# Sums of weights pinned behind the work written ahead of them, in a float32 encoder that multiplies by Strassen's scheme

## The chip, the cores and the metric

The kernel runs on one core of a Trainium2 chip. The metric is the device time of one execution in microseconds. A core has five engines that work through queues of their own, in the order in which the program lists their instructions, and meet only at semaphores: TensorE (PE, matmuls; its weight loads are shown as PEld), VectorE (DVE), ScalarE (ACT), GpSimd (POOL) and SyncE (SP, which here only issues DMAs). TensorE accumulates in PSUM; all else lives in SBUF.

## The reference

Two token groups (256 and 512 tokens, width 1024) go through the same two layers in float32. A layer is

```
x <- LN1(alpha*x + 0.5*SwiGLU_1(x))
x <- LN2(alpha*x + W_out[ attention(x) | ssd(x) ])
x <- LN3(alpha*x + 0.5*SwiGLU_2(x))
SwiGLU(x) = (silu(x @ w_gate) * (x @ w_up)) @ w_down      # 1024 -> 2816 -> 1024
```

The middle step has neighbourhood attention and a bidirectional state-space scan. The change touches only the four SwiGLU blocks, which take most of the time.

## The kernel before

**Precision.** A float32 product is made of three faster ones. Each operand is cut into a high part (a cast to fp32r) and a low part (what is left), and high x high, high x low and low x high are added in PSUM. `parts` cuts a block of weights: ScalarE casts the high half (L101 or L105); the low half is made by VectorE (L106) or, where `acc` is set, by ScalarE writing minus the high half (L102) and a DMA from POOL's queue that adds the raw block to it (L103). A cut block lies in one of twelve places, w0 to w4 for gate and up, w5 to w11 for down.

**Pairs.** The 2816 hidden columns are worked in eleven pairs of 128-column tiles. `plain_pair` does the first. `fast_pair` does the other ten by a Strassen scheme: seven products of quarter matrices for gate (m=0) and seven for up (m=1) instead of eight each, in the order of `PRODUCTS`. A product is twelve matmuls of 128x384 at L524. Three of the seven use raw quarters of the weights (0, 1, 3) and four use sums of them, S1 to S4, which `WeightStream.source` makes on VectorE at L89 (S1 = 2+3, S2 = S1-0, S3 = 0-2, S4 = 1-S2) into one of three temporary blocks. On the side of x the partners are quarters of x (XH, XL) and sums of those (T1 to T4 with halves T2h, T2l and so on). A product's weights are cut four products ahead: `ws.get(1, NGU-1)`.

After the last product `finish` makes sums of the hidden quarters (L445 to L448) and `put_h` cuts them (L434 on ScalarE, L436 on VectorE) into h0 to h6.

**Down.** In pairs 1 to 8 the down projection goes by the same scheme, one pair late: `down_units` has 21 runs (three column blocks of seven products, in the order h0, h1, h3, h4, h6, h5, h2), and `fast_pair` of the next pair does one or two behind each of its products. A run is three matmuls of 128x512 (L596) and one or two accumulations into y on VectorE (L599). h0, h4, h5 and h2 share one bank of PSUM (psB), h3 and h6 another (psC): h4's matmuls wait until VectorE has read h0's result, h6's until it has read h3's. `down_step` makes the weights of down: T1, T3, T2 and -T4 are sums in place in the raw blocks (L126, L130, L128, L132), and seven casts cut them, the last of them (into w11) the block that -T4 left.

**Raw weights.** They come in halves of a slab, 512 KB a DMA on SP's queue (L71), into four buffers `wraw`: for each pair two halves of gate, two of up, two of down. A load starts when its buffer's last reader is done.

**Who sets the order.** The kernel is written in program order, and a scheduler then sets the order of each engine's queue. It keeps all dependencies, and among instructions that have none it goes by its own estimate of when operands are ready; it also hands out the buffers of `wraw`. So a sum whose weights it takes to have landed can come ahead of work that is written before it.

Of the kernel before, what the change touches and what calls it, by code (L numbers as in the profile page):

```python
# [36 lines left out]
UNIT = 512  # L37
# [13 lines left out]
class WeightStream:  # L51
# [7 lines left out]

    SUMS = {"S1": (2, "add", 3), "S2": ("S1", "sub", 0), "S3": (0, "sub", 2), "S4": (1, "sub", "S2")}  # L60

    def __init__(self, nc, pool, halves, units, temps, places):
        self.nc, self.pool, self.halves, self.units, self.temps, self.places = nc, pool, halves, units, temps, places
        self.raw, self.sums = {}, {}
        self.ndma = self.nsplit = self.nget = self.nsum = 0
# [14 lines left out]
    def source(self, u, what, n):  # L80
        if not isinstance(what, str):
            return self.block(u["at"][what], n)
        key = (u["at"][0], what)
        if key not in self.sums:
            a, op, b = self.SUMS[what]
            a, b = self.source(u, a, n), self.source(u, b, n)
            out = self.temps[self.nsum % len(self.temps)]
            self.nsum += 1
            (self.nc.vector.tensor_add if op == "add" else self.nc.vector.tensor_sub)(out, a, b)  # L89
            self.sums[key] = out  # L90
        return self.sums[key]

# [28 lines left out]
    def down_step(self, half, step):  # L121

        b11, b12, b21, b22 = (self.block((half + k // 2, k % 2)) for k in range(4))
        sub = self.nc.vector.tensor_sub
        if step == "T1":
            sub(b11, b12, b11)  # L126
        elif step == "T3":
            sub(b12, b22, b12)  # L128
        elif step == "T2":
            sub(b11, b22, b11)  # L130
        elif step == "-T4":
            sub(b21, b21, b11)  # L132
        else:
            hl = self.parts((b11, b21, b11, b11, b22, b12, b21)[step], NGU + step, acc=step not in (0, 2))
            if step >= 5:
                self.dma(half + step - 1)
            return hl
# [9 lines left out]
def trunk(ctx, tc, x_in, w_gu, w_dn, w_xbc, w_z, w_qk, w_v, w_out, ln_gb, ln_gbc, conv_wb, gmix, smalls, bias, y_out):  # L147
    nc = tc.nc
# [3 lines left out]
    wpool = ctx.enter_context(tc.tile_pool(name="wpool", bufs=1))  # L152
# [10 lines left out]
    def at(off, n, dt=F32):  # L163
        a = arena[:, off : off + n]
        return a if dt == F32 else a.bitcast(dt)
# [28 lines left out]
    o_sum, o_s, o_sg = 24 * KB, 30 * KB, 36 * KB  # L194
# [3 lines left out]
    halves, units = [], []  # L198
# [77 lines left out]
                u["place"] = NGU + k if k < NDN else NGU - 1  # L276
            ring[0] = NGU - 1 if w == 1 else NW - 1
    wt = [pers.tile([P, 2 * ZN], F32R, name=f"w{i}") for i in range(NW)]
    ws = WeightStream(nc, wpool, halves, units, [at(o_sum + i * UNIT, UNIT) for i in range(3)], wt)

    y = at(o_y, NT * DM).rearrange("p (t d) -> p t d", t=NT)
    gb = at(o_gb, 2 * DM).rearrange("p (s d) -> p s d", s=2)
# [959 lines left out]
```

## Time and profile before

| | us |
|---|---|
| median of 3 runs | 2982.32 |
| lowest, highest | 2973.87, 2982.59 |
| the profiled execution's own time | 2994.69 |
| its span | 2992.5 |
| TensorE busy | 2883.1 |
| VectorE busy | 2191.0 |
| ScalarE busy | 1583.4 |

The profile is of one execution. Busy time is a union over an engine's instructions; a matmul's end is modelled, so TensorE's share is no measure of its speed. The timeline view gives start, duration, engine, line and operation; in square brackets stands how long the engine had been idle before and what ended that. In the windows view PEclk is the granted share of TensorE's clock (1.00 is 2.4 GHz, 0.50 is 1.2 GHz).

### The profile page before, as it was taken

What the parts mean: (1) busy time and instruction counts of PE and PEld (TensorE: products, weight loads), DVE (VectorE), ACT (ScalarE), POOL (GpSimd) and SP (SyncE); (2) the same over time, 40 slices, a digit from 0 to 9 for tenths busy, and PEclk for the clock granted to TensorE, in tenths of its full rate; (3) what the DMA queues carried; (4) which work ended last, traced back from release to release, by engine and by line L of the source; (5) the groups of instructions that cost most, each with busy time, mean ns of one, the idle gap of its engine ahead of it and who ended that gap; (6) DMA issues with size and microseconds to landing.
All of it is one profiled execution on the core that took longest, in us unless ns stands there. A gap on an engine that the chain in (4) does not pass through costs nothing.

```text
span 2992.5 us, 41957 instructions
## 1 busy us (share of the span) xinstructions
PE 2883.1 (96%) x15094; PEld 2534.0 (85%) x15094; DVE 2191.0 (73%) x4207; ACT 1583.4 (53%) x3231; POOL 408.8 (14%) x513
## 2 busy tenths in 40 slices
PE   8999999999999999999989999999999999999998
PEld 7988889888767888888979888898887778888897
DVE  7777777768435877777797778877783458887877
ACT  4645454657345455554545455545573464554543
POOL 2112120100000211121031121200000002121210
PEclk9999999999889999999999999999997999999999
DMA  3555453224323255554215554632343233454642
GB/s 122 126 121 126 114 127 114 99 88 137 111 62 125 81 134 110 128 128 112 85 36 122 125 126 114 140 100 102 99 124 114 76 122 92 113 132 109 135 106 77
DMA packets 128880, 330.26 MB, mean 110 GB/s; under 512 B 14816, under 2 KB 27296, under 8 KB 127904
## 3 DMA queue, kind: packets, MB, share of 16 engines
q1 hardware_dynamic: 82592, 243.68, 25.6%
q0 software_dynamic: 46080, 83.91, 16.4%
q8 instruction: 118, 1.93, 0.3%
q14 instruction: 90, 0.74, 0.1%
HBM read 224.67 MB, written 18.97 MB: 81 GB/s over the span
## 4 chain that ended last, share of the span: by engine, by line
PE 71%; DVE 11%; DMA 7%; issue 6%; POOL 3%; ACT 2%; POOLq 0%; DVEq 0%; SPq 0%; ACTq 0%
PE psA L524 28%; PE psB L596 7%; PE psA L1119 5%; PE psA L407 5%; PE psA L965 5%; PE psC L596 4%; DMA w<-wraw 4%; DMA wraw<-in_w_gu_dram 3%; PE psB L1054 3%; PE psB L618 3%; PE psC L618 3%; PE psA L772 2%; PE psA L992 2%; DVE arena L599 2%; PE psC L1083 2%
## 5 line engine op out<-in xcount | busy, mean ns | idle before, releaser
L524 PE MATMUL psA<-XH,w 128*128 128x384 f32 x2560 | 700.4, 338 | 5.3 <-DMA w<-wraw 5.3
L524 PEld LDWEIGHTS psA<-XH,w 128*128 128x128 f32 x2560 | 468.6, 188 | 14.4 <-DMA w<-wraw 6.6
L103 POOL DMA_DIRECT2D w<-wraw x320 | 273.8, 881 | 1322.9 <-ACT w L102 1168.0
L524 PE MATMUL psA<-XL,w 128*128 128x384 f32 x1280 | 432.6, 338 | 0.0
L105 ACT CAST w<-arena 128x512 fp32r<-128x512 f32 x320 | 198.4, 620 | 390.2 <-PE psA L524 357.4
L105 ACT CAST w<-wraw 128x512 fp32r<-128x512 f32 (+1 forms) x320 | 194.6, 620 | 214.4 <-PE psA L524 103.9
L106 DVE TENSOR_TENSOR w<-wraw,w 128x512 fp32r<-128x512 f32 (+1 forms) x320 | 216.0, 688 | 110.1 <-ACT w L105 106.3
L599 DVE SCALAR_TENSOR_TENSOR arena<-psB,arena 128x512 f32<-128x512 f32 x384 | 260.7, 686 | 45.5 <-PE psB L596 45.5
L106 DVE TENSOR_TENSOR w<-arena,w 128x512 fp32r<-128x512 f32 x320 | 219.6, 687 | 66.4 <-ACT w L105 66.4
L524 PEld LDWEIGHTS psA<-XL,w 128*128 128x128 f32 x1280 | 240.7, 188 | 7.5
L101 ACT CAST w<-wraw 128x512 fp32r<-128x512 f32 x320 | 197.4, 618 | 92.8 <-PE psA L524 56.5
L407 PE MATMUL psA<-XH,w 128*128 128x256 f32 (+1 forms) x1056 | 241.5, 335 | 5.0 <-DVE XH L372 5.0
L102 ACT ACTIVATE w<-w 128x512 fp32r<-128x512 f32 x320 | 198.8, 631 | 5.7
L599 DVE SCALAR_TENSOR_TENSOR arena<-psC,arena 128x512 f32<-128x512 f32 x288 | 191.7, 684 | 3.3
L407 PEld LDWEIGHTS psA<-XH,w 128*128 128x128 f32 x1056 | 168.6, 189 | 27.0 <-DVE XH L372 6.3
L524 PE MATMUL psA<-T4h,w 128*128 128x384 f32 x640 | 183.6, 348 | 0.0
L524 PE MATMUL psA<-T3h,w 128*128 128x384 f32 x640 | 181.1, 344 | 0.0
L524 PE MATMUL psA<-T2h,w 128*128 128x384 f32 x640 | 177.4, 338 | 0.0
L89 DVE TENSOR_TENSOR arena<-wraw 128x512 f32<-128x512 f32 x160 | 109.4, 686 | 91.9 <-DMA wraw<-in_w_gu_dram 81.6
L539 DVE TENSOR_TENSOR arena<-arena,psA 128x384 f32<-128x384 f32 x240 | 132.0, 550 | 56.9 <-PE psA L524 50.3
L330 POOL TENSOR_TENSOR stat<-stat,cst 128x1 f32<-128x1 f32 x60 | 25.7, 429 | 1033.2 <-ACT arena L933 415.7
L407 PE MATMUL psA<-XL,w 128*128 128x256 f32 (+1 forms) x528 | 151.1, 335 | 2.0 <-DVE XL L373 2.0
(359 smaller groups left out, 6356.0 us busy)
## 6 DMA issues: line engine op xcount, KB each, us to landing
wraw<-in_w_gu_dram SPq DMA_DIRECT2D x176, 512.0 KB, 3.8
w<-wraw POOLq DMA_DIRECT2D x320, 256.0 KB, 4.1
wraw<-in_w_dn_dram SPq DMA_DIRECT2D x88, 512.0 KB, 3.7
e<-ac_d SPq DMA_DIRECT2D x48, 256.0 KB, 3.3
wraw<-in_w_xbc_dram SPq DMA_DIRECT2D x16, 512.0 KB, 4.7
wraw<-in_w_qk_dram SPq DMA_DIRECT2D x16, 512.0 KB, 3.9
arena<-in_bias_dram SPq DMA_DIRECT2D x64, 128.0 KB, 2.1
wraw<-in_w_out_dram SPq DMA_DIRECT2D x16, 512.0 KB, 4.2
```

Of the source, the lines that this page charges most:

```text
L101: nc.scalar.copy(hi, raw)
L102: nc.scalar.activation(lo, hi.bitcast(F32), AF.Copy, scale=-1.0)
L103: nc.gpsimd.dma_start(lo, raw, accum_op=ALU.add)
L105: nc.scalar.copy(hi, raw)
L106: nc.vector.tensor_sub(lo, raw, hi.bitcast(F32))
L407: t_.matmul(ps[:, o : o + b - a], w[:, k % 4], xx[:, k, a:b], start=(k == 0 and part == 0 and i == 0), stop=(k == KD - 1 and part == 1))
L524: t_.matmul(ps, wx[:, k], xx[:, k], start=first and k == 0 and i == 0, stop=k == 3 and i == 2, skip_group_check=not first)
L596: t_.matmul(ps, hx, wx, start=first and k == 0, stop=k == 2, skip_group_check=not first)
L599: v_.scalar_tensor_tensor(sl, ps, 0.5, sl, op0=ALU.mult, op1=ALU.add)
L618: t_.matmul(ps[n], hx, units[2 * i + n][wx], start=(i == 0 and wi == 0), stop=(i == nf - 1 and wi == 2))
L965: t_.matmul(ps[r][:, : b - a], w[:, k % 4], xx[:, k, a:b], start=(k == 0 and part == 0 and i == 0), stop=(k == KD - 1 and part == 1))
L1119: t_.matmul(p[n], xx[:, k, cols], wo[2 * k + n][wx], start=(i == 0 and wi == 0), stop=(i == KD - 1 and wi == 2))
```

## The change

Two kinds of VectorE instruction get one edge more: every sum of weights (L89) and the sum -T4 (L132). The edge, `keep_in_program_order`, puts the instruction behind the one that was traced before it on VectorE. It is an order of issue and adds no wait. Nothing is added or left out, each engine has the same instructions as before, and lines from 63 on have a number one higher.

```diff
-    def __init__(self, nc, pool, halves, units, temps, places):
+    def __init__(self, tc, pool, halves, units, temps, places):
+        nc, self.in_order = tc.nc, tc.keep_in_program_order
...
-            (self.nc.vector.tensor_add if op == "add" else self.nc.vector.tensor_sub)(out, a, b)
+            self.in_order((self.nc.vector.tensor_add if op == "add" else self.nc.vector.tensor_sub)(out, a, b))
...
-            sub(b21, b21, b11)
+            self.in_order(sub(b21, b21, b11))
...
-    ws = WeightStream(nc, wpool, halves, units, [at(o_sum + i * UNIT, UNIT) for i in range(3)], wt)
+    ws = WeightStream(tc, wpool, halves, units, [at(o_sum + i * UNIT, UNIT) for i in range(3)], wt)
```

The scheduler's order follows from it. Below, `arena` holds the temporary sums, the hidden sums and y; numbers at the end of a name are those of the built program. wraw_2704 and wraw_2730 are the halves of gate (m=0) of pair 7 in the first SwiGLU block, wraw_2869 and wraw_2894 those of up (m=1), wraw_2532 and wraw_2551 those of down of pair 6.

VectorE's queue at the end of pair 6, before:

```order
L543 TENSOR_TENSOR arena_66<-arena_66 128x384
L89 TENSOR_TENSOR arena_66<-wraw_2730,arena_66 128x512
L445 TENSOR_TENSOR arena_66<-arena_66 128x384
L89 TENSOR_TENSOR arena_66<-wraw_2869,wraw_2894 128x512
L446 TENSOR_TENSOR arena_66<-arena_66 128x384
L436 TENSOR_TENSOR h3l_186<-arena_66,h3h_185 128x384
L447 TENSOR_TENSOR arena_66<-arena_66 128x384
L436 TENSOR_TENSOR h5l_190<-arena_66,h5h_189 128x384
L448 TENSOR_TENSOR arena_66<-arena_66 128x384
L436 TENSOR_TENSOR h4l_188<-arena_66,h4h_187 128x384
L539 TENSOR_TENSOR arena_66<-arena_66,psA_2928 128x384
L436 TENSOR_TENSOR h6l_192<-arena_66,h6h_191 128x384
```

The same place now, up to the first accumulation of a down run:

```order
L544 TENSOR_TENSOR arena_66<-arena_66 128x384
L446 TENSOR_TENSOR arena_66<-arena_66 128x384
L447 TENSOR_TENSOR arena_66<-arena_66 128x384
L448 TENSOR_TENSOR arena_66<-arena_66 128x384
L437 TENSOR_TENSOR h3l_186<-arena_66,h3h_185 128x384
L449 TENSOR_TENSOR arena_66<-arena_66 128x384
L437 TENSOR_TENSOR h4l_188<-arena_66,h4h_187 128x384
L437 TENSOR_TENSOR h5l_190<-arena_66,h5h_189 128x384
L437 TENSOR_TENSOR h6l_192<-arena_66,h6h_191 128x384
L90 TENSOR_TENSOR arena_66<-wraw_2704 128x512
L540 TENSOR_TENSOR arena_66<-arena_66,psA_2928 128x384
L600 SCALAR_TENSOR_TENSOR arena_66<-psB_2948,arena_66 128x512
```

S4 of m=0 (wraw_2730) and S1 of m=1 (wraw_2869, wraw_2894) have left the middle of `finish`; S3 of m=0 stands behind it, S4 some rows further, S1 and S2 of m=1 behind the seventh accumulation.

VectorE's queue some rows earlier, at the end of the product T4 of pair 6, before:

```order
L132 TENSOR_TENSOR wraw_2551<-wraw_2551,wraw_2532 128x512
L89 TENSOR_TENSOR arena_66<-wraw_2704 128x512
L539 TENSOR_TENSOR arena_66<-arena_66,psA_2789 128x384
L599 SCALAR_TENSOR_TENSOR arena_66<-psB_2750,arena_66 128x512
L543 TENSOR_TENSOR arena_66<-arena_66 128x384
L106 TENSOR_TENSOR w0_89<-arena_66,w0_89 128x512
L599 SCALAR_TENSOR_TENSOR arena_66<-psB_2750,arena_66 128x512
L543 TENSOR_TENSOR arena_66<-arena_66,psA_2699 128x384
```

The same place now:

```order
L540 TENSOR_TENSOR arena_66<-arena_66,psA_2789 128x384
L600 SCALAR_TENSOR_TENSOR arena_66<-psB_2750,arena_66 128x512
L544 TENSOR_TENSOR arena_66<-arena_66 128x384
L107 TENSOR_TENSOR w0_89<-arena_66,w0_89 128x512
L600 SCALAR_TENSOR_TENSOR arena_66<-psB_2750,arena_66 128x512
L437 TENSOR_TENSOR h2l_184<-arena_66,h2h_183 128x384
L544 TENSOR_TENSOR arena_66<-arena_66,psA_2699 128x384
L133 TENSOR_TENSOR wraw_2551<-wraw_2551,wraw_2532 128x512
```

-T4 (L132, now L133) has moved behind the block of the product T4 (psA_2699) and h2's low half, and S3 is gone from this stretch.

SP's queue with the semaphores that each load waits for, before. DMAHW lanes are given to SP's loads in turn, 0 to 7, so the lane that a load waits for tells which earlier load had its buffer:

```order
L71 DMA wraw_2704<-in_w_gu_dram 128x1024 [waits DMASW0_49,DMAHW0_49,DVE_49,Activation_49]
L71 DMA wraw_2730<-in_w_gu_dram 128x1024 [waits DMAHW1_49,DMASW1_49,DVE_49]
L71 DMA wraw_2869<-in_w_gu_dram 128x1024 [waits DMASW2_49,DMAHW4_49,DVE_49,Activation_49]
L71 DMA wraw_2894<-in_w_gu_dram 128x1024 [waits DMASW7_49,DMAHW2_49,DMASW6_49,Activation_49]
L71 DMA wraw_2913<-in_w_dn_dram 128x1024 [waits DMASW5_49,DMAHW3_49,DMASW0_49,Activation_49]
```

The same loads now:

```order
L72 DMA wraw_2704<-in_w_gu_dram 128x1024 [waits DMASW0_49,DMAHW0_49,DVE_49,Activation_49]
L72 DMA wraw_2730<-in_w_gu_dram 128x1024 [waits DMAHW1_49,DMASW1_49,DVE_49]
L72 DMA wraw_2869<-in_w_gu_dram 128x1024 [waits DMASW7_49,DMASW5_49,DMAHW2_49,DVE_49,Activation_49]
L72 DMA wraw_2894<-in_w_gu_dram 128x1024 [waits DMASW6_49,DMAHW3_49,DMASW0_49,Activation_49]
L72 DMA wraw_2913<-in_w_dn_dram 128x1024 [waits DMAHW4_49,DMASW2_49,DVE_49]
```

wraw_2704 has lane 4, so wraw_2869 has lane 6 and took the buffer of wraw_2704, two loads back; now it takes that of lane 2, wraw_2532, four back. wraw_2894 took that of wraw_2532 and now takes that of wraw_2551 (lane 3); wraw_2913 took that of wraw_2551 and now takes that of wraw_2704.

TensorE's queue has the same matmuls. In the pairs with down runs, T4 of m=0 now follows h5 directly, and the run h2 stands behind seven matmuls of T4, where it stood behind eight (m=0) and ten (m=1).

## Rows read from the trace of the kernel before

**Rows 1.** The page, part 1: engine, busy time, share, instructions.

```profile
PE 2883.1 (96%) x15094; PEld 2534.0 (85%) x15094; DVE 2191.0 (73%) x4207; ACT 1583.4 (53%) x3231; POOL 408.8 (14%) x513
```

**Rows 2.** Waits of TensorE: who waited for whom, total, times, longest.

```profile
PE psB L596 <- DVE arena L599: 23.8, 32, 1.3
PE psC L596 <- DVE arena L599: 23.5, 28, 0.9
...
PE psC L596 <- DVE h3l L436: 9.4, 10, 2.2
```

**Rows 3.** Waits of VectorE.

```profile
DVE arena L89 <- DMA wraw<-in_w_gu_dram: 81.6, 28, 5.3
```

**Rows 4.** Timeline of VectorE, 342 to 354: start, duration, instruction, idle before.

```profile
343.56 0.55 DVE L445 TENSOR_TENSOR arena<-arena 128x384 f32<-128x384 f32 x1
347.23 0.69 DVE L89 TENSOR_TENSOR arena<-wraw 128x512 f32<-128x512 f32 x1 [3.12 <-DMA wraw<-in_w_gu_dram]
347.84 0.55 DVE L446 TENSOR_TENSOR arena<-arena 128x384 f32<-128x384 f32 x1
...
349.25 0.55 DVE L436 TENSOR_TENSOR h5l<-arena,h5h 128x384 fp32r<-128x384 f32 x1
...
351.58 0.68 DVE L599 SCALAR_TENSOR_TENSOR arena<-psB,arena 128x512 f32<-128x512 f32 x1
```

**Rows 5.** Timeline of TensorE, 349 to 356: the product T1, h4 and h6.

```profile
349.25 0.34 PE L524 MATMUL psA<-XH,w 128*128 128x384 f32 x1
...
351.16 0.34 PE L524 MATMUL psA<-XH,w 128*128 128x384 f32 x1
352.42 0.70 PE L596 MATMUL psB<-w,h4h 128*128 128x512 f32 x2 [0.92 <-DVE arena L599]
...
354.21 0.70 PE L596 MATMUL psC<-w,h6h 128*128 128x512 f32 x2 [0.86 <-DVE arena L599]
```

**Rows 6.** Timeline of TensorE, 343 to 393: h0 of two pairs that follow each other.

```profile
344.82 0.62 PE L596 MATMUL psB<-w,h0h 128*128 128x512 f32 x2
345.27 0.40 PE L596 MATMUL psB<-w,h0l 128*128 128x512 f32 x1
...
392.39 0.62 PE L596 MATMUL psB<-w,h0h 128*128 128x512 f32 x2
```

**Rows 7.** Windows: length, busy time by engine (instructions), PEclk, DMA share, GB/s.

```profile
207.20:210.60 3.40, 3.33 (x10) 2.30 (x8) 3.40 (x7) 3.37 (x7) 0.46 (x1) 0.50 0.27 102
344.82:392.39 47.57, 45.26 (x232) 40.85 (x232) 37.32 (x65) 25.36 (x48) 8.53 (x11) 1.00 0.54 120
2746.70:2750.10 3.40, 3.40 (x12) 3.29 (x11) 1.71 (x3) 0.00 (x0) 0.19 (x1) 0.51 0.90 160
```

**Rows 8.** Timeline of VectorE, 382 to 392.

```profile
382.69 0.69 DVE L132 TENSOR_TENSOR wraw<-wraw 128x512 f32<-128x512 f32 x1 [1.22 <-DMA w<-wraw]
...
386.71 0.54 DVE L543 TENSOR_TENSOR arena<-arena,psA 128x384 f32<-128x384 f32 x1
```

**Rows 9.** Timeline of ScalarE, 381 to 396: a copy, a cast and its scaling.

```profile
382.05 0.46 ACT L534 COPY arena<-psA 128x384 f32<-128x384 f32 x1
...
386.82 0.62 ACT L101 CAST w<-wraw 128x512 fp32r<-128x512 f32 x1
387.47 0.64 ACT L102 ACTIVATE w<-w 128x512 fp32r<-128x512 f32 x1
```

**Rows 10.** Timeline of POOL's queue, 376 to 396.

```profile
388.40 0.84 POOL L103 DMA_DIRECT2D w<-wraw  x1 [3.02 <-PE psA L524]
```

**Rows 11.** The chain of waits, in order of time: start, length, what.

```profile
391.57 4.25 DMA wraw<-in_w_gu_dram
...
426.96 4.16 DMA w<-wraw
...
2728.64 6.37 DMA w<-wraw
```

## The prediction, made before the changed kernel was run

> **What bounds the kernel now.** I read part 1 of the page, the waits of TensorE and VectorE, the timeline of one pair on both, the windows at low clock, and the chain of waits. TensorE is busy for 2883.1 us of 2992.5 and VectorE for 2191.0 [rows 1]: the end is set by TensorE's stream, so a change on VectorE pays only where TensorE waits for it. It does wait: 23.8 us in 32 waits and 23.5 us in 28 for VectorE's accumulation into y (L599), and 9.4 us in 10 for a low half that VectorE makes (L436) [rows 2]. All three are matmuls of the line that runs down's units inside a fast pair (L596).
>
> Why VectorE is late there stands in its own waits: 28 times a sum of weights (L89) sat until a DMA of a gate/up slab had landed, 81.6 us together, 5.3 at most [rows 3]. One pair shows it. After the first block of `finish` (L445, 343.56) the next instruction in VectorE's queue is S1 of the coming units. Its transfer lands 3.12 us later, and L446 to L448, the low halves and the first L599 stand behind it: that L599 starts at 351.58 [rows 4]. TensorE needs its end before h4. The product before h4 ends its stream at 351.16, h4 starts at 352.42 with 0.92 us idle, h6 at 354.21 with 0.86 [rows 5]. The view counts idle time from a modelled matmul end; from start to start h4 comes 1.26 us after a matmul that takes its turn every 0.17 us, so 1.08 us are lost where 0.92 is shown, some 0.17 more for each wait.
>
> The pair as a whole: from h0 of one to h0 of the next, 344.82 to 392.39, are 47.57 us [rows 6]. Its work is 168 matmuls of L524 and 63 of L596. Twelve of the first start between 349.25 and 351.16 [rows 5], 0.174 us apart; the first and the third of h0 at 344.82 and 345.27 [rows 6], 0.225 apart. That makes 29.2 + 14.2 = 43.4. So 4.2 us a pair are lost at most, and with 28 such pairs 117 us is the most that can come back.
>
> **The change part by part.** *S1 and S2 of the second matrix (m=1).* They move from the middle of `finish` to behind h2's accumulation, some 20 rows later. No instruction is added. What was held: L446 to L448 no longer stand behind a transfer. In the pair of [rows 4], L539 and L543 are followed at once by L445; I take 0.47 us from start to start, as between 347.84 and its followers up to 349.25. Eight instructions end near 346.1, plus about 0.9 for high halves that ScalarE must cast between them (an estimate, two turns of 0.47): 347.0. Then S3, one block, and h0's L599 are done near 348.7 (0.6, 0.47, 0.6); h4 wants it at 351.3, 2.6 us of room where it was 0.9 late. Behind it stand a low half, S4, and two L599, four times 0.6: 351.1, and h6 wants that at 352.0, 0.9 of room. The low half of h3 (9.4 us of waits) moves 3 us forward too. So all three rows of [rows 2] go: 23.8 + 23.5 + 9.4 = 56.7, plus 0.17 for each of their 70 waits, 11.9: 68.6 us.
>
> *S3 and S4 of both matrices.* They now follow `finish` and the L599 they were written behind. S3 of m=0 feeds the fifth product (T3): sum near 347.6, cast and low half 1.3 us later, wanted after h6, near 352.7. Hidden, with 3 us of room; were that gone, T3 would wait for each us.
>
> *The clock.* Five times in this execution the granted clock fell to 0.50 for 3.4 us, from 207.2 to 2746.7, each right after these waits in a fast pair; the first and the last stand in [rows 7]. 1.2 instead of 2.4 GHz over 3.4 us costs 1.7 us, 8.5 together. The same waits stand in 28 pairs and only five had a fall, so it may be less in another execution. I count 8.5.
>
> The Trainium skill, TensorE: Matmul & The Clock Gate, Part 1, has the low clock as the default that activity lifts and an idle stretch brings back. By that, no waits means no falls and the whole 8.5; by the rows, where 23 of 28 pairs had the waits and no fall, anything from 0 to 8.5, which moves the sum to 60 at the least.
>
> *-T4 (L132).* It stood at 382.69, behind a 1.22 us wait for a DMA. It now stands behind L543 of the product T4, which cannot start before that product ends: 386.71 in [rows 8], so it ends near 387.9, 4.5 us later. The cast of `down`'s last unit waits for it; that cast was at 386.82 anyway, because its place w11 is free only after h2, and its DMA was issued from POOL's queue at 388.40 [rows 9, 10]. So the issue slips from 388.4 to about 389.3, 0.9 us. VectorE gains: that wait and S3 leave the stretch ahead of h5's L599, for which h2 waited in some pairs (part of the 32 waits).
>
> *The four raw buffers.* They are handed out in the new order as well: the loads keep their order on SP's queue, but each now takes the buffer four loads back. The second half of m=1 waits for the last accumulating DMA of down's last unit, where it waited for the unit before, and the load of down's first half waits for S3. Accumulating DMAs on the chain take from 4.16 to 6.37 us, the load of half a slab 4.25 in this pair [rows 11]. So this half is issued at 393.5 to 395.7 instead of 391.57 and lands at 397.7 to 400. It is first needed by a cast on ScalarE after the product T1. In a pair without waits that is 392.39 plus h0, T2, h1, h3 and T1 (0.68 + 2.09 + 1.35 + 2.09): 398.6. That cast and its scaling (0.62 and 0.64, [rows 9]) must be over when T3 ends, after 1.35 + 2.09 more, 402.0, since the copy behind them frees T4's bank. So up to 400.8 a late half costs TensorE nothing, and behind that each us costs a us. Cost: 0, with 0.8 to 3.1 us of room. S1 itself runs near 405 and finds its operand there.
>
> The Trainium skill, DMA: Bandwidth & Descriptors, Anatomy of one DMA, gives 2.0 us plus bytes/436e3 in us for DMAs that POOL issues. For 256 KB that is an estimate of 2.6 us, and the half would be issued near 391.9, as early as now; the trace disagrees with 4.16 to 6.37, so the room is counted from the trace.
>
> *TensorE's order.* T4 now follows h5 directly (two matmuls of h0 stood between), and h2 comes after seven matmuls of T4 instead of eight or ten. T4 needs a copy out of its bank, 0.46 us on ScalarE [rows 9], that starts when T3 has ended; h5's three matmuls cover 0.68. h2 needs h5's L599, which stands behind one block. Between 0 and 0.5 us a pair for both; with h6's narrow room I take 0.3, 28 times: 8 us.
>
> **The sum.** 68.6 + 8.5 - 8 = 69 us. Against the profiled execution, 2994.69, that is 2926. That execution is 12.4 us above the median of the runs, 2982.32; the waits belong to the program and not to one execution, so 2982 - 69 = 2913.
>
> **Rivals.** *The ring of buffers becomes the bound (slower).* Place: SP's load of the second half of m=1, now behind -T4, cast, scaling, accumulating DMA and its own transfer. It decides from a landing at 400.8 in the pair above. At 404 all 3 us a pair are eaten and the time is 2982; at 405 it is 1 us x 28 more, 3010. For it: the chain is longer than before. Against: from 389.3 the longest pieces shown, 6.37 and 4.25, end at 400. Half of it, 2 us late, leaves 69 - 56 = 13 us of gain: 2969.
>
> *VectorE is too full (no change).* Its work per pair stays while the pair shrinks, from 37.3 of 47.6 us [rows 7] to 37.3 of some 44.5. Then L599 of h0, h3 and h5 are late for another reason: some 2 us at h4 and h6 would return, 28 x 2 = 56, and with the 8 the time is about 2975; with the falls of the clock too, 2982. For it: over eight tenths in use, in strict order. Against: the delay was one wait of 3 us ahead of a chain [rows 4], not a backlog.
>
> *The sums stay where they were.* The order of the changed program excludes it: S1 stands behind seven accumulations.
>
> **How the numbers follow.** The waits go: 0.74, 2913, own range 2880 to 2945 (from 102 us, most of what a pair loses, to 37, with no clock term and the allowance at 1.1 us a pair). The ring half late: 0.09, 2969. VectorE too full: 0.09, 2975 to 2982. The ring late by over 3 us: 0.08, 3010. What a measurement of this kernel tells from no change is about 0.3%, 9 us. Faster 0.74 + 0.09 = 0.83, same 0.09, slower 0.08. The range, 2880 to 2968, leaves out the slow case, most of VectorE's, and part of the ring's.
>
> **What would show it.** In the changed kernel: no wait of L89 for a gate/up DMA of 28 times 3 us; TensorE's waits for L599 and for h3's low half under 15 us in all; h0 to h0 near 44.5 us; L446 to L448 in a row. For the ring: ScalarE's cast of a raw block (L101, one line on) waiting for a gate/up DMA, and T4's weights waiting for the copy. For VectorE: h4 and h6 still waiting for L599 with VectorE busy without a gap before it. I am wrong if the pair takes 47 us again, whatever the waits are called.

## The result, and the profile after

| | before | changed |
|---|---|---|
| median of the first comparison, us | 2978.10 | 2895.44 |
| lowest, highest | 2958.52, 2982.59 | 2893.69, 2896.72 |
| ratio, 95% interval | | 0.9734, 0.9689 to 0.9780 |
| the same kernel again, in another job on the chip | 2975.67 | 2884.12 |
| ratio, 95% interval | | 0.9692, 0.9628 to 0.9755 |

2.7 to 3.1% faster: 83 and 92 us. The forecast was 2913, 69 us.

Executions of one kernel lie up to 55 us apart here, and the granted clock explains most of it. TensorE is busy 96 to 98% of the span, so span times mean granted clock is about what the execution would take at full clock. For the kernel before the median of that product is 2927, 2929 and 2930 in three jobs (7, 23 and 7 executions); for the changed kernel 2856 and 2859 (4 and 4). So 68 to 74 us are work and waits (68 in the one job that has the clocks of both), and the rest of the 83 and 92 is time at the low clock. Below, "at full clock" means the median of this product. Within a job it spreads over 5 to 14 us from one execution to the next, so differences of a few us are not resolved.

The page of the changed kernel, part 1 (busy time, share, instructions), stands against [rows 1]:

```profile
PE 2837.5 (98%) x15094; PEld 2521.1 (87%) x15094; DVE 2210.1 (76%) x4207; ACT 1580.4 (55%) x3231; POOL 408.5 (14%) x513
```

TensorE's waits, longest first. The three rows of [rows 2], 56.7 us, have no counterpart in the whole list, and the first three here stood before with 19.2, 5.0 and 5.3 us:

```profile
PE psB L619 <- ACT h1h L435: 19.7, 4, 7.5
PE psA L408 <- DVE XH L373: 5.0, 3, 1.7
PE psA L525 <- DMA w<-wraw: 5.0, 4, 1.6
```

VectorE's wait of [rows 3], 81.6 us in 28 times, has shrunk to:

```profile
DVE arena L90 <- DMA wraw<-in_w_gu_dram: 4.5, 3, 2.6
```

The pair that answers to [rows 4 to 6]. VectorE's timeline (start, duration, idle before in brackets): the four sums of `finish` and the low halves run without a gap, and h0's L600 starts at 335.23, 2.65 us after h0's first matmul (332.58), where L599 started 6.76 us after it (344.82 to 351.58).

```profile
329.96 0.56 DVE L446 TENSOR_TENSOR arena<-arena 128x384 f32<-128x384 f32 x1
330.55 0.56 DVE L447 TENSOR_TENSOR arena<-arena 128x384 f32<-128x384 f32 x1
331.14 0.56 DVE L448 TENSOR_TENSOR arena<-arena 128x384 f32<-128x384 f32 x1
331.62 0.55 DVE L437 TENSOR_TENSOR h3l<-arena,h3h 128x384 fp32r<-128x384 f32 x1
...
335.23 0.68 DVE L600 SCALAR_TENSOR_TENSOR arena<-psB,arena 128x512 f32<-128x512 f32 x1
...
337.04 1.28 DVE L600 SCALAR_TENSOR_TENSOR arena<-psC,arena 128x512 f32<-128x512 f32 x2
```

TensorE's timeline: h4 and h6 follow the product T1 and each other with no idle time, and the next pair's h0 comes at 377.00.

```profile
332.58 0.62 PE L597 MATMUL psB<-w,h0h 128*128 128x512 f32 x2
...
338.70 0.34 PE L525 MATMUL psA<-XH,w 128*128 128x384 f32 x1
338.88 0.63 PE L597 MATMUL psB<-w,h4h 128*128 128x512 f32 x2
339.34 0.40 PE L597 MATMUL psB<-w,h4l 128*128 128x512 f32 x1
339.58 0.64 PE L597 MATMUL psC<-w,h6h 128*128 128x512 f32 x2
...
377.00 0.62 PE L597 MATMUL psB<-w,h0h 128*128 128x512 f32 x2
```

From h0 to h0 are 44.42 us, 3.15 less than in [rows 6]. The 28 steady pairs together (seven in each SwiGLU block, from h0 to h0) took 1317.1 us before, of which 17.1 at the low clock, and 1243.9 now: 73.2 us less. The five falls account for 8.5 of it, so the waits for 64.7, 2.3 us a pair. The window of that pair (length, busy by engine, PEclk):

```profile
332.63:377.05 44.42, 44.42 (x233) 41.19 (x232) 37.88 (x66) 25.27 (x49) 8.57 (x10) 1.00 0.57 130
```

VectorE has 37.88 us of work in 44.42, and TensorE waits for none of it. In this profile, and in that of the second job, the clock fell in no steady fast pair; [rows 7] had two of five such falls. What is left of low clock lies outside, most of it in one stretch of attention and the start of the output projection.

### The profile page after: what moved, and what is told of

The parts are those of the page before. It is cut to its first block, busy times and chain, and to the rows that moved or that the text cites. A ratio compares the mean times of both kernels' runs of the same rounds, so it can differ in the third digit from the quotient of the medians.

```text
span 2894.8 us, 41895 instructions
## 1 busy us (share of the span) xinstructions
PE 2837.5 (98%) x15094; PEld 2521.1 (87%) x15094; DVE 2210.1 (76%) x4207; ACT 1580.4 (55%) x3231; POOL 408.5 (14%) x513
## 4 chain that ended last, share of the span: by engine, by line
PE 86%; DVE 6%; ACT 3%; DMA 2%; issue 2%; POOL 1%; DVEq 0%; SPq 0%; POOLq 0%; ACTq 0%
PE psA L525 37%; PE psB L597 9%; PE psC L597 7%; PE psA L408 5%; PE psA L1120 5%; PE psA L966 5%; PE psB L619 3%; PE psC L619 3%; PE psB L1055 3%; PE psA L773 2%; PE psA L993 2%; PE psC L1084 2%; DMA wraw<-in_w_dn_dram 1%; PE psB L1073 1%; DVE w L107 1%
## 5 line engine op out<-in xcount | busy, mean ns | idle before, releaser
L600 DVE SCALAR_TENSOR_TENSOR arena<-psB,arena 128x512 f32<-128x512 f32 x384 | 260.4, 685 | 63.6 <-PE psB L597 62.1
L102 ACT CAST w<-wraw 128x512 fp32r<-128x512 f32 x320 | 195.2, 619 | 139.6 <-PE psA L525 64.3
L600 DVE SCALAR_TENSOR_TENSOR arena<-psC,arena 128x512 f32<-128x512 f32 x288 | 191.6, 683 | 7.7
L535 ACT COPY arena<-psA 128x384 f32<-128x384 f32 x240 | 113.4, 473 | 82.5 <-PE psA L525 82.5
```

Source lines behind the costliest of these rows:

```text
L102: nc.scalar.copy(hi, raw)
L600: v_.scalar_tensor_tensor(sl, ps, 0.5, sl, op0=ALU.mult, op1=ALU.add)
```

## The experiments

All have the line numbers of the changed kernel unless said. "Pinned" means the edge that the change adds. "Measured" is the time over that of the kernel before in the same job, with its 95% interval.

**Which move pays.** Four kernels in one job.

Sums alone, -T4 free (sums_only):

```diff
-            self.in_order(sub(b21, b21, b11))
+            sub(b21, b21, b11)
```

> Only the sums of weights (L90) are pinned; -T4 is free again and stands where it stood before the change. Theory (S1 of m=1 inside finish was the whole loss): no wait of L90 for a gate/up DMA, pairs of 44.4 us from h0 to h0, 2893 to 2905 us, as with the full change. Rival (moving -T4 matters too, by freeing VectorE ahead of h5's accumulation and h2): h2 and h5 wait again, some 0.5 us a pair, 2910 or more.

Measured: 0.9825 (0.9781 to 0.9868), at full clock 2874. Steady pairs take 44.4 us, up to 45.6 in a few. The waits for L600 are gone but for 2.2 us; a new one is there, four times:

```profile
PE psA L525 <- DMA w<-wraw: 21.0, 4, 5.7
```

So both theories missed: -T4 is worth some 16 us at full clock, but neither at h5 nor at h2.

-T4 alone (t4_only):

```diff
-            self.in_order((self.nc.vector.tensor_add if op == "add" else self.nc.vector.tensor_sub)(out, a, b))
+            (self.nc.vector.tensor_add if op == "add" else self.nc.vector.tensor_sub)(out, a, b)
```

> Only -T4 is pinned; S1 of m=1 stands in the middle of finish again, one instruction later than before the change. Theory: L90 waits for the DMA of the second half of m=1 some 28 times by about 3 us, pairs of 47 us, 2955 to 2985 us as before the change. Rival (-T4's place was half of the loss): 2930.

Measured: 1.0077 (1.0044 to 1.0110), 0.8% slower than the kernel before. At full clock it is 2933, only 4 us more; the rest is time lost at the low clock, a median of 66 us against 48. TensorE's three waits are all there, the low half's larger than in [rows 2]:

```profile
PE psB L597 <- DVE arena L600: 25.0, 28, 0.9
PE psC L597 <- DVE arena L600: 24.6, 29, 0.9
PE psC L597 <- DVE h3l L437: 20.2, 28, 2.2
```

S1 and S2 of the second matrix alone (m1_only; `u["m"]`, the unit's matrix, is stored by a line that is not shown):

```diff
-            self.in_order((self.nc.vector.tensor_add if op == "add" else self.nc.vector.tensor_sub)(out, a, b))
+            (self.in_order if u["m"] == 1 and what in ("S1", "S2") else (lambda i: i))((self.nc.vector.tensor_add if op == "add" else self.nc.vector.tensor_sub)(out, a, b))
...
-            self.in_order(sub(b21, b21, b11))
+            sub(b21, b21, b11)
```

> Only S1 and S2 of the second matrix (m=1) are pinned; S3 and S4 of both matrices and -T4 are free, and S4 of m=0 stands ahead of finish. Theory: that one move carries the gain, 2893 to 2910 us, pairs of 44.4 to 44.8. Rival (VectorE is too full, any block ahead of finish makes h4 and h6 late): 2930 to 2950, with TensorE's waits for L600 back in part.

Measured: 0.9815 (0.9767 to 0.9863), at full clock 2868: 61 of the 68 to 74 us. In the steady pairs the raw buffers are handed out as in the kernel before, so the new ring order is not what pays. Of the rest, the wait for a DMA into w in four places is 14.0 us.

The wait put back, in the full change, by code written in another place (wait_back; the line that stores `u["m"]` is not shown):

```diff
-            v_.tensor_add(a22, a21, a22)
+            nxt = [u for u in ws.units[ws.nsplit - 1 :] if "m" in u][:14]
+            for m, what in ((0, "S3"), (0, "S4"), (1, "S1")):
+                if what == "S1":
+                    v_.tensor_add(a22, a21, a22)
+                for u in nxt:
+                    if u["m"] == m:
+                        ws.source(u, what, UNIT)
+                        break
             v_.tensor_sub(a21, a11, a21)
```

> The full change, with one thing undone by writing it so: S3 and S4 of m=0 stand ahead of finish and S1 of m=1 in the midst of it, all still pinned. Theory: S1 waits for its DMA again, 2 to 4 us in some 28 pairs, h4 and h6 wait for L600 (here L607), pairs of 46.5 to 48 us, 2950 to 2990. Rival (the gain comes from the new order of the raw buffers or from -T4): the wait is there but the time stays near 2895 to 2910.

Measured: 0.9982 (0.9942 to 1.0022), at full clock 2926, where the kernel before has 2927 to 2930. VectorE waits and TensorE behind it (lines 7 higher):

```profile
DVE arena L90 <- DMA wraw<-in_w_gu_dram: 80.0, 35, 3.6
```

```profile
PE psC L604 <- DVE arena L607: 37.2, 28, 1.3
PE psB L604 <- DVE arena L607: 21.1, 30, 1.8
```

Three sums in other places, of which S1 is the one that waits, take the whole gain back: 58.3 us in 58 waits as shown, 68 with the 0.17 that each of them lost above what was shown. S4 stands ahead of `finish` in m1_only too, at no such cost. The raw buffers are not held fixed here: the second half of m=1 takes the buffer three loads back, neither the order of the changed kernel nor that of the kernel before. But m1_only gains with the order of before, and this kernel loses with another, so it is the wait that goes with the time in both. This profile also has the pairs' clock falls again, 15 of them; one as a window (the 0.50 is the clock):

```profile
1179.10:1182.50 3.40, 3.27 (x9) 3.01 (x10) 1.27 (x2) 0.00 (x0) 0.43 (x1) 0.50 0.86 149
```

**Where -T4 pays.** In sums_only the four waits stand at the start of the second fast pair of each SwiGLU block. The chain of waits there, in order of time (start, length, what), sums alone and then the changed kernel:

```profile
97.22 7.68 DMA w<-wraw
104.90 0.04 issue
104.94 7.13 PE psA L525 x24
```

```profile
99.13 3.31 DMA w<-wraw
102.44 0.04 issue
102.48 8.15 PE psA L525 x45
```

The accumulating DMA makes the low half of that pair's first product. With -T4 free, -T4 runs in the first fast pair at 87.39 instead of 105.87, its raw buffers come free, and SP has issued four loads by 98.00 where the changed kernel has issued two. The last two, 512 KB each, are issued at 97.20 and 97.63 and run beside the DMA, and the 256 KB take 7.68 us instead of 3.31. SP's timeline, sums alone and then the changed kernel (start, length from the first issue to the last, how many):

```profile
90.41 7.59 SPq L72 DMA_DIRECT2D wraw<-in_w_gu_dram  x4
```

```profile
91.02 3.10 SPq L72 DMA_DIRECT2D wraw<-in_w_gu_dram  x2
```

The Trainium skill, DMA: Bandwidth & Descriptors, "Issuing engines are not separate DMA queues", says that DMAs of different engines interleave on the same DMA engines. The two lengths agree: 7.68 us beside the loads, 3.31 without them. And as the wait ends the clock falls:

```profile
104.00:110.80 6.80, 5.86 (x18) 5.86 (x19) 0.65 (x2) 0.69 (x2) 0.00 (x0) 0.50 0.19 35
```

Such a fall stands at all four places, 23.9 us in all, so some 12 us more that the figure at full clock leaves out.

Three kernels test it. -T4 pinned in the first fast pair only (t4_first):

```diff
-    def down_step(self, half, step):
+    def down_step(self, half, step, pin=False):
...
-            self.in_order(sub(b21, b21, b11))
+            (self.in_order if pin else (lambda i: i))(sub(b21, b21, b11))
...
-                        hl = ws.down_step(half, step)
+                        hl = ws.down_step(half, step, p == 1)
```

> All sums pinned, and -T4 pinned only in the first fast pair of each SwiGLU block (4 places instead of 32). Theory (the free -T4 costs only there: it frees the raw buffers early, two 512 KB loads then run beside the accumulating DMA that makes the weights of the next pair's first product, which takes 7.7 us instead of 3.3): TensorE's wait of 5.4 us, four times, is gone, time as with the full change, 2893 to 2902 us. Rival (the free -T4 costs in every pair): nearer to 2921, as with the sums alone.

Measured: 0.9763 (0.9705 to 0.9821), at full clock 2860, as the full change. So 4 of the 32 pins of -T4 carry what it is worth.

Sums alone, and the first two blocks of the second fast pair cut by VectorE (sums_noacc):

```diff
-acc = not isinstance(x, str) and 1 < p < NPAIR - 1 and (m, x) != (1, 3)
+acc = not isinstance(x, str) and 1 < p < NPAIR - 1 and (m, x) != (1, 3) and (p, m, x) not in ((2, 0, 0), (2, 0, 1))
```

> Sums pinned, -T4 free, and the first two blocks of the second fast pair (m=0, quarters 0 and 1) get their low halves from VectorE instead of from an accumulating DMA. Theory (TensorE waits there for that DMA, slowed by two loads beside it): no wait for a DMA into w there, 2893 to 2905 us against 2921. Rival (the load or ScalarE's cast of the block is late as well): the wait stays above 3 us, 2912 or more.

Measured: 0.9752 (0.9678 to 0.9825), median 2907, at full clock 2866. The wait for the DMA is gone, half of the 16 us comes back, and a wait takes its place: T4 for ScalarE's copy (L535), 9.1 us in 12 in the whole kernel, where the changed one has 3.8 in 5. Between the two expectations: the DMA was late, and the work behind it too.

The same edit on the full change (after_noacc):

> The full change, and the same two blocks cut by VectorE. The changed kernel still waits 5.0 us in four places for that DMA. Theory: they go, 3 to 5 us less, 2890 us. Rival (VectorE's two more instructions, 0.7 us each, push h0 or a sum back there): 2895 to 2900.

Measured: 0.9674 (0.9619 to 0.9729), at full clock 2856 against 2859 for the changed kernel in that job. The 5.0 us of waits are gone. Its median, 2871, is 13 us under the changed kernel's 2884, but the clock gave most of that (0.995 and 0.996 in three of four executions). It beats the kernel before; that it beats the changed one is not shown.

**The two rivals.** *VectorE too full.* Three or six more instructions in `finish`, each a block's maximum with itself:

```diff
     v_.tensor_add(a22, a21, a22)
-    v_.tensor_sub(a21, a11, a21)
+    for _ in range(3):
+        ws.in_order(v_.tensor_tensor(a22, a22, a22, op=ALU.max))
+    ws.in_order(v_.tensor_sub(a21, a11, a21))
```

> The full change, and three more VectorE instructions in every finish (a block's maximum with itself, 128x384, which changes nothing; some 1.4 us of VectorE and 1.8 us of the chain behind it). Theory (VectorE has room: in the changed kernel h0's accumulation ends 2.9 us and h3's 1.2 us ahead of h4 and h6, and h3's moves up a row here): pairs stay at 44.4 to 44.6 us, 2873 to 2902 us. Rival (VectorE is nearly full): 1 to 1.4 us more in each of 28 pairs, 30 to 40 us more.

Measured: 0.9694 (0.9632 to 0.9756), at full clock 2860, pairs 44.4 us. VectorE's busy time is 2257.5, 47 us more than in the changed kernel, and nothing of it shows.

> Six of them: 2.8 us of VectorE, 3.5 us of the chain, about the length of the wait that the change took away. Theory: the room is used up; h6 and the product T3 come 0.5 to 1.5 us late, 14 to 42 us over the changed kernel, with TensorE's waits for L600 (here L603) or for VectorE's low halves back. Rival (only a DMA's wait hurts, work that stands there does not): no change.

Measured: 0.9761 (0.9673 to 0.9848), at full clock 2863. The median is 2912, at granted clocks of 0.978 to 0.986 in three of four executions; the low clock of the profile lies outside the steady pairs. These take 44.5 to 45.4 us, 7.4 us more than in the changed kernel for all 28, with no wait for VectorE's accumulation anywhere: VectorE is busy 2295.9, 86 us more, for 4 to 7 us of time. I had expected 14 to 42. Six such instructions are work that the scheduler can reckon with, and the order differs: h0's accumulation now stands between them (334.80 in VectorE's timeline), where the wait of S1 had it behind itself. That this is the reason is argued, not shown.

```profile
334.33 0.55 DVE L448 TENSOR_TENSOR arena<-arena 128x384 f32<-128x384 f32 x1
334.80 0.69 DVE L602 SCALAR_TENSOR_TENSOR arena<-psB,arena 128x512 f32<-128x512 f32 x1
335.40 0.55 DVE L448 TENSOR_TENSOR arena<-arena 128x384 f32<-128x384 f32 x1
```

*The ring of buffers.* -T4 one product later, and -T4 with the cast behind it after `finish`:

```diff
-        STEPS = {8: (0,), 9: (1, "T1", "T3"), 10: (2,), 11: ("T2", 3, 4), 12: ("-T4", 5), 13: (6,)}
+        STEPS = {8: (0,), 9: (1, "T1", "T3"), 10: (2,), 11: ("T2", 3, 4), 12: (5,), 13: ("-T4", 6)}
```

```diff
-        STEPS = {8: (0,), 9: (1, "T1", "T3"), 10: (2,), 11: ("T2", 3, 4), 12: ("-T4", 5), 13: (6,)}
+        STEPS = {8: (0,), 9: (1, "T1", "T3"), 10: (2,), 11: ("T2", 3, 4), 12: (5,)}
...
             finish(p)
+            if half is not None:
+                ws.down_step(half, "-T4")
+                dnw[p].append(ws.down_step(half, 6))
```

> The full change with -T4 one product later. It frees the raw buffer that the second half of m=1 is loaded into, some 2.8 us later. Theory (room of the buffer ring: in the changed kernel the cast of that half is over 1.7 us before ScalarE has to copy T4's bank): 1.1 us a pair, some 30 us more than the changed kernel; TensorE waits for the copy (L535) ahead of T4. Rival (there is more room, the half is not needed so early): within 10 us.

> -T4 and the cast behind it after finish, some 7 us later than in the changed kernel. Theory: the half lands 7 us later, 1.7 of them hidden: 5 us in each of 28 pairs, 140 us more, slower than before the change (3000 to 3050). Rival (more room or a shorter chain): 2900 to 2960.

Measured: 0.9773 (0.9697 to 0.9850), at full clock 2862, and 0.9718 (0.9655 to 0.9782), at full clock 2860; most steady pairs take 44.4 us in both. Of the first 30 us were expected and 3 to 6 came, of the second 140 and 1 to 4. The first has a median of 2912, at granted clocks of 0.981 to 0.984 in three of four executions, and again the low clock of its profile lies outside the steady pairs. ScalarE's timeline at the disputed cast (L102), in one pair each of the changed kernel, of -T4 one product later and of -T4 at the end:

```profile
339.58 0.62 ACT L102 CAST w<-wraw 128x512 fp32r<-128x512 f32 x1 [1.71 <-DMA wraw<-in_w_gu_dram]
340.23 0.63 ACT L103 ACTIVATE w<-w 128x512 fp32r<-128x512 f32 x1
342.59 0.48 ACT L535 COPY arena<-psA 128x384 f32<-128x384 f32 x1 [1.73 <-PE psA L525]
```

```profile
384.95 0.63 ACT L102 CAST w<-wraw 128x512 fp32r<-128x512 f32 x1 [2.45 <-DMA wraw<-in_w_gu_dram]
385.61 0.63 ACT L103 ACTIVATE w<-w 128x512 fp32r<-128x512 f32 x1
387.13 0.48 ACT L535 COPY arena<-psA 128x384 f32<-128x384 f32 x1 [0.89 <-PE psA L525]
```

```profile
385.48 0.62 ACT L102 CAST w<-wraw 128x512 fp32r<-128x512 f32 x1
386.13 0.63 ACT L103 ACTIVATE w<-w 128x512 fp32r<-128x512 f32 x1
387.22 0.48 ACT L535 COPY arena<-psA 128x384 f32<-128x384 f32 x1 [0.45 <-PE psA L525]
```

In these pairs the copy waits for TensorE, with 1.73, 0.89 and 0.45 us of room. The median over the fast pairs with down runs is 1.87, 0.30 and 0.46: the half comes some 1.5 us later in both, not 2.8 and 7. With -T4 at the end the buffers were handed out in another order again: the half takes the buffer of the load three back, which S3 frees, and not the one that -T4 holds.

In a few pairs the half is really late. The worst is one of -T4 one product later, with h0 at 1049.01; ScalarE's timeline, then TensorE's:

```profile
1059.45 0.62 ACT L102 CAST w<-wraw 128x512 fp32r<-128x512 f32 x1 [3.50 <-DMA wraw<-in_w_gu_dram]
1060.10 0.63 ACT L103 ACTIVATE w<-w 128x512 fp32r<-128x512 f32 x1
1060.64 0.46 ACT L535 COPY arena<-psA 128x384 f32<-128x384 f32 x1
```

```profile
1061.15 0.44 PE L525 MATMUL psA<-T4h,w 128*128 128x384 f32 x1 [1.49 <-ACT arena L535]
```

The copy starts 11.63 us after h0, where 10.0 is usual, and the pair takes 46.00 us instead of 44.4. TensorE waits for this copy in four pairs of that kernel (0.25 to 1.49 us) and in five of -T4 at the end (0.26 to 1.12). So a us of lateness behind the room does cost about a us; it is met in too few pairs to show in the time.

## Why the prediction came out as it did

*The place of the loss* was right: S1 of m=1 waiting inside `finish`. m1_only brings 61 us by taking it out, wait_back loses 67 to 71 by putting it in, t4_only keeps it and gains nothing. The chain came out as reckoned too: h0's L600 ends 2.97 us ahead of h4 (2.6 forecast) and h3's 1.26 ahead of h6 (0.9).

*68.6 us for the waits* was right: 68 to 74 at full clock and 64.7 in the steady pairs, all three rows gone, pairs of 44.42 where "near 44.5" stood. The floor of 43.4 us a pair was 1 us too low, since pairs without these waits take 44.42, and so the 117 us that could come back at most were too many. *The 8 us of new small waits* were the mis-sized term: the waits for L600 and for h3's low half, 15 us allowed, are absent, and T4's copy, one of the two that made the 0.3 us a pair, is waited for 3.8 us in 5 times. Of the 14 and 23 us that the result is better than the forecast, these are some 8; the rest is mostly the clock.

*8.5 us for the clock*: the falls in steady pairs, 17.1 us at the low clock before, are gone in the two profiles of the changed kernel and back in that of wait_back (47.8 us), as the term said. What else the clock did the forecast lacked. The time lost at low clock (span times one minus clock) has a median of 45 to 48 us before and of 36 and 23 after, 8 to 25 less. In the profiles the difference beyond the falls is one long stretch (below), worth 20 us: the kernel before has two, the changed one has one. Whether that belongs to the change cannot be said from eight executions.

*S3 and S4 at no cost*: right, TensorE waits for no sum. *The ring*: its landing time was right (in the pair above the cast starts 7.0 us after h0, on the landing, and 5.3 to 7.6 was forecast), and so was the price, a us for each us late. The sign that was named for it, ScalarE's cast waiting for a gate/up DMA, does stand in the changed kernel, and costs TensorE next to nothing:

```profile
ACT w L102 <- DMA wraw<-in_w_gu_dram: 43.0, 27, 3.0
```

Two prices of the rivals do not follow from the prediction's own terms. The 69 us are eaten by a half that is 2.5 us late, a landing near 403.3 and not 404. And 2 us at h4 and h6 leave 13 of the 69, 2969, or 2978 without the clock, where 2975 and 2982 stand.

*-T4 at no cost* is the step that was right in the total and wrong in its reason, so that its total came out was luck. I followed it through a steady pair, where it slips by under a us and costs nothing. In the first fast pair, which I had not looked at, it keeps two loads away from a DMA that TensorE waits for. The kernel before did not have that wait (0.8 us there, 5.3 in all four places), so nothing was gained on it; the sums alone bring it on, and -T4 takes it off again.

## What to carry to other kernels

Look first at what an in-order engine has standing behind an instruction that waits for a DMA: the scheduler orders by its own estimate of the landing, and 3 us of error ahead of a chain cost 2.3 us of TensorE a pair, while 2.8 us of work in the same place cost 0.3. Follow a moved step through the first and the last turn of a loop too, and ask which transfers it lets start early. And compare kernels whose clock wanders at equal clock (span times granted clock): its medians agreed within 3 us in three jobs of one kernel, whose single times lay up to 55 apart.

## What the runs showed of the chip

One long stretch at 1.2 GHz, in attention and the start of the output projection, comes or does not in executions of one and the same program. The changed kernel's profile has it in the second layer and not at the same place of the first; that of after_noacc has it in neither, that of the kernel before in both. Windows of the changed kernel, of after_noacc and of the kernel before:

```profile
772.00:816.00 44.00, 42.99 (x216) 29.18 (x216) 18.04 (x73) 22.47 (x63) 1.48 (x4) 1.00 0.36 113
...
2202.00:2246.30 44.30, 44.15 (x120) 28.43 (x120) 10.11 (x43) 12.87 (x39) 0.74 (x2) 0.50 0.26 84
```

```profile
2197.30:2241.30 44.00, 43.61 (x218) 29.73 (x218) 16.96 (x69) 21.99 (x61) 1.48 (x4) 1.00 0.35 111
```

```profile
794.30:838.70 44.40, 44.36 (x120) 28.43 (x120) 10.23 (x43) 12.79 (x38) 0.74 (x2) 0.50 0.26 84
2285.90:2326.90 41.00, 41.00 (x112) 26.14 (x111) 9.32 (x40) 11.72 (x36) 0.74 (x2) 0.50 0.27 86
```

In 44 us TensorE does 218 matmuls at the one level and 120 at the other; each such stretch costs 20 us or so, as much as the step between the executions of one kernel (2873.66, 2875.97, 2892.26 and 2893.64 for the changed one in its second job; the 3 us between the four of the first were chance). What lets it start or not is not known. And a 256 KB accumulating DMA took 3.31 us with no load beside it and 7.68 beside two of 512 KB and the end of a third.
